# A decoder layer on one Trainium2 core: the forget gate's projection as eight unsplit fp32 products in column groups, and one vector sum moved in the opening

## The chip, the cores and the metric

The kernel runs on one core of one Trainium2 chip. A core has a matrix engine (PE, with its weight loads listed apart as PEld), a vector engine (DVE), a scalar engine (ACT), a general engine (POOL) and a sync engine (SP), which here only issues DMA transfers. The engines run side by side, each through its own queue of instructions in order, and wait for each other by semaphores. The metric is the device time of one execution in microseconds (us).

## What is computed

One decoder layer on 512 tokens of width 1024. A conditioning vector gives six modulation vectors; the token-mixing half applies one combined input projection to the modulated input `u`, runs two causal attention branches of eight heads each, merges and projects them; a gated MLP with a causal convolution follows. The part that matters here is the head of the layer:

```python
mod = c @ w_ada + b_ada
sh1, sc1, gt1, sh2, sc2, gt2 = [m[:, None, :] for m in jnp.split(mod, N_MOD, axis=-1)]
u = x * (1.0 + sc1) + sh1
proj = u @ w_in
q_a, k_a, v_a, f_a, q_b, k_b, v_b, g_a, g_b = jnp.split(proj, _split_points(), axis=-1)
log_f = jax.nn.log_sigmoid((f_a + b_forget).astype(jnp.float32)).transpose(0, 2, 1)
```

`f_a` is the forget gate: eight columns of the projection, one per head of the forgetting attention. Its logarithm is summed along the sequence and enters the logits of that branch, which is the second of the two to run.

## The kernel before, in words

**Products.** Every fp32 product is made of three products of a faster four-byte type, fp32r. An operand is split into a high part (a copy to fp32r on ACT, `hi_of`) and a low part (operand minus high part on DVE, `lo_of`), and the three are high by high, high by low and low by high. A stationary operand of 128 columns and a moving one of 512 make one product of shape 128x512 in one of the eight banks of PSUM.

**The opening** (lines 222 to 383) runs over eight tiles `j` of 128 rows of the contraction. For each tile, SP issues (`first_load`) two blocks of modulation weights `wa[0]`, `wa[1]` of 128x1024, the input weights `r` of 128x904, and the transposed input `xt` of 128x512. `first_acc` makes the tile's shift and scale: `mod_col` multiplies a weight block by the broadcast vector `cbc` and sums it in one DVE instruction (line 241), reads the accumulator, and adds the bias (line 247). `first_mod` then makes `u`: twice on ACT (line 318 into the high part `uh`, line 323 in place into `xt`, unsplit), and `ul = xt - uh` on DVE; the low part `wl` of the weights, 904 columns, is made on DVE just ahead of that. `first_split` makes the high part of the next tile's weights on ACT.

Of the 904 weight columns, seven groups of 128 go to banks `grp[0]` to `grp[6]`: query and key of a first pair of heads and five gate blocks. The last eight columns are the forget gate. `first_pad` splits them once more into a zeroed tile `fpad` of 128 columns per tile: the high part in columns 0 to 7, the low part in columns 64 to 71. `first_ops` then needs two full-width products for them, `fpad` by `uh` and `fpad` by `ul`, both into `grp[7]`. So a tile has 7 x 3 + 2 = 23 products (line 361), and the opening 184.

**The order on PE in the opening** follows `first_mm`: groups 0 to 4, then 5 to 7; in the last tile groups 2, 0, 1, then 7, then 3 to 6. On DVE the explicit order (`issue_after`) per tile is: sum 0 and sum 1 of the tile (`first_acc`), `wl`, `ul`, the low part into `fpad`; the next tile's sums stand behind that. Between other instructions of an engine the order comes from a scheduler that places what it takes to be ready, so an instruction of a later line can stand ahead of one of an earlier line; SP's order is the program's.

**After the opening**, `q_evac` and `k_evac` split the first pair's query and key out of the banks. `forget_evac` (line 405) takes the forget gate out: rows 64 to 71 of `grp[7]` by an ACT copy, then rows 0 to 7 plus the bias plus that copy by DVE, into `fq[1]`. `forget` (line 409) is issued in the loop over heads before the second branch's attention (line 839): an absolute value, an exponential and a logarithm on ACT, a minimum and a running sum on DVE, then a split, and its rows go to the heads by DMAs of POOL. The rest of the projection follows in 128-column blocks, three products for each tile of the contraction (`proj`, `mm3`, lines 152 to 154), mixed with the attention of the heads.

**Buffers.** `xt`, `uh`, `ul`, `fq` and most tiles of the attention come from one pool of 58 tiles of 128x512 (`z`). The modulation weights have five buffers, `r` five, the split weights three.

Of the kernel before, what the change touches and what calls it, by code (L numbers as in the profile page):

```python
# [8 lines left out]
F32 = mybir.dt.float32  # L9
F32R = mybir.dt.float32r  # L10
BF16 = mybir.dt.bfloat16
AF = mybir.ActivationFunctionType
ALU = mybir.AluOpType
# [3 lines left out]
P = 128  # L17
T = 512
D = 1024
KT = D // P  # L20
# [5 lines left out]
NH = 8  # L26
# [25 lines left out]
def layer_kernel(ctx: ExitStack, tc: tile.TileContext, out, xT, x, c8, wa0, wa1, bcol, w1, wct, wv, bf,  # L52
# [3 lines left out]
    V, S, G, PE = nc.vector, nc.scalar, nc.gpsimd, nc.tensor  # L56
# [12 lines left out]
    early = st0.enter_context(tc.tile_pool(name="early", bufs=1))  # L69

    cnt, state = [0], {"load": 0, "proc": 0}

    def nm(s):
        cnt[0] += 1
        return f"{s}_{cnt[0]}"

    def bank():
        return pp.tile([P, 512], F32, name=nm("ps"), tag="ps")
# [5 lines left out]
    def const(shape, dt, s):  # L84
        return cons.tile(shape, dt, name=s, tag=s)

    def fl(ap):
        return ap.bitcast(F32)

    def hi_of(o, i, scale=1.0):  # L90
        S.activation(o, i, AF.Copy, scale=scale)

    def lo_of(o, i, hi):
        state["read"] = V.tensor_tensor(o, i, fl(hi), ALU.subtract)  # L94
        return state["read"]
# [33 lines left out]
    g = G.tensor_copy(crow[0:KT], c8s)  # L129
# [11 lines left out]
    bfs = const([NH, 1], F32, "bfs")  # L141
# [6 lines left out]
    def z(dt, s, shape=(P, 512)):  # L148
        return zp.tile(list(shape), dt, name=nm(s), tag="z", bufs=NZ)
# [73 lines left out]
    grp = [bank() for _ in range(8)]  # L223
    pend = {}

    fpad = early.tile([P, KT, P], F32R, name="fpad", tag="fpad")
    with tc.issue_after(g.ins):
        G.memset(fl(fpad), 0.0)
    def heat(n):
        return [PE.matmul(grp[5], warm[:, 0:P], warm, start=True, stop=True) for _ in range(n)]  # L230

    heat(WARM[0])
    for k in range(KT):
        o = grp[6 + k // 4][:, k % 4 * P : (k % 4 + 1) * P]
        m = PE.matmul(o, sel[:, k : k + 1].broadcast_to([P, P]), ctop, start=True, stop=True)
# [8 lines left out]
    def mod_col(w, col, wt):  # L244
        mod_sum(w, col, wt, slice(0, D), 0)
        b, o = bcols[:, w, col : col + 1], modc[:, w, col : col + 1]
        return V.tensor_tensor(o, modr[:, w, col, 0:1], b, ALU.add)
# [25 lines left out]
    def first_acc(j):  # L273
        wa = pend[j][0]
        if j == 0:
            s = state["chl"]
            for e in range(2):
                for q in range(2):
                    c = slice(q * 512, (q + 1) * 512)
                    with tc.issue_after(s.ins):  # L280
                        s = mod_sum(q, j, wa[e], c, e, grp[6 + e])
                    if e or q:
                        for m in heat(WARM[2] + e * q):
                            paced(m, s)
                    if e and not q:
                        with tc.issue_after(s.ins):
                            s = V.tensor_tensor(bcols[:, 0:2, j], bcols[:, 0:2, j], modr[:, 0:2, j, 0], ALU.add)
            with tc.issue_after(s.ins):
                state["modc"] = V.tensor_tensor(modc[:, 0:2, j], modr[:, 0:2, j, 1], bcols[:, 0:2, j], ALU.add)
        else:  # L290
            mod_col(0, j, wa[0])
            state["modc"] = mod_col(1, j, wa[1])

    def first_split(j):
# [9 lines left out]
    def first_pad(j):  # L304
        h, l, r = pend[j][2:]
        if j == 0:
            c = slice(384, W1C)
            lo_of(l[:, c], r[:, c], h[:, c])
        f = slice(W1C - NH, W1C)
        hi_of(fpad[:, j, 0:NH], r[:, f])  # L310
        state["after"] = lo_of(fpad[:, j, 64 : 64 + NH], r[:, f], h[:, f])

    def first_mod(j):
        wa, xt = pend[j][0:2]
        sh, sc = modc[:, 0, j : j + 1], modc[:, 1, j : j + 1]
        a, b = z(F32R, "uh"), z(F32R, "ul")
        if j:
            u = S.activation(a, xt, AF.Identity, bias=sh, scale=sc)
            h, l, r = pend[j][2:]
            with tc.issue_after(state["modc"].ins):  # L320
                state["after"] = lo_of(l[:, 0:W1C], r[:, 0:W1C], h[:, 0:W1C])
            with tc.issue_after(u.ins):
                u = state["u"] = S.activation(xt, xt, AF.Identity, bias=sh, scale=sc)
            with tc.issue_after(state["after"].ins):
                state["after"] = lo_of(b, xt, a)
        else:
            h, l, r = pend[j][2:]
            with tc.issue_after(state["modc"].ins):
                ts = V.tensor_scalar(a, x0, sc, sh, ALU.mult, ALU.add)
            with tc.issue_after(state["h"].ins):  # L330
                u = S.activation(xt, x0, AF.Identity, bias=sh, scale=sc)
            c = slice(384, W1C)
            with tc.issue_after(u.ins):
                u = S.activation(h[:, c], r[:, c], AF.Copy)
            for e in range(2):
                with tc.issue_after(u.ins):
                    u = state["u"] = S.activation(cbc[:, e * 512 : (e + 1) * 512], grp[6 + e], AF.Copy)
            with tc.issue_after(ts.ins):
                ts = lo_of(l[:, 0:384], r[:, 0:384], h[:, 0:384])
            with tc.issue_after(ts.ins):  # L340
                state["after"] = lo_of(b, xt, a)
        with tc.issue_after(u.ins), tc.issue_after(state["after"].ins):
            first_pad(j)
        uh.append(a)
        ul.append(b)

    def first_ops(j, g):
        h, l = pend[j][2:4]
        a, b = uh[j], ul[j]
        if g == 7:  # L350
            return [(fpad[:, j, :], a), (fpad[:, j, :], b)]
        c = slice(g * P, (g + 1) * P)
        return [(h[:, c], a), (l[:, c], a), (h[:, c], b)]

    def first_mm(j, gs):
        ops = [(g, n, m) for g in gs for n, m in enumerate(first_ops(j, g))]
        if j < KT - 1:
            rank = (0, 2, 4, 1, 3, 5)
            ops.sort(key=(lambda o: rank[o[1]] + 3 * (o[0] > 2) if o[0] < 5 else o[1] + 3 * (o[0] == 7)) if j == 0 else lambda o: o[1] + 3 * (o[0] == 7))
        for g, n, (w, u) in ops:  # L360
            PE.matmul(grp[g], w, u, start=j == 0 and n == 0, stop=j == KT - 1 and n == (1 if g == 7 else 2))  # L361

    for j in range(2):
        first_load(j)
    first_split(0)
    first_acc(0)
    first_mod(0)
    for j in range(KT):
        if j + 2 < KT:
            first_load(j + 2)  # L370
        if j + 1 < KT:
            with tc.issue_after(state["u"].ins):
                first_split(j + 1)
            with tc.issue_after(state["after"].ins):
                first_acc(j + 1)
        if j < KT - 1:
            first_mm(j, range(5))
        if j + 1 < KT:
            first_mod(j + 1)
        if j < KT - 1:  # L380
            first_mm(j, range(5, 8))
        else:
            first_mm(j, (2, 0, 1, 7, 3, 4, 5, 6))

    st0.close()

# [14 lines left out]


    fq = [z(F32, "fq", (NH, 512)) for i in range(2)]

    def forget_evac():
        S.activation(fq[0], grp[7][64 : 64 + NH, :], AF.Copy)
        V.scalar_tensor_tensor(fq[1], grp[7][0:NH, :], bfs, fq[0], ALU.add, ALU.add)

    def forget(after):
        with tc.issue_after(after.ins):  # L410
            S.activation(fq[0], fq[1], AF.Abs)
            S.activation(fq[0], fq[0], AF.Exp, scale=-1.0)
            S.activation(fq[0], fq[0], AF.Ln, bias=1.0)
        V.scalar_tensor_tensor(fq[1], fq[1], 0.0, fq[0], ALU.min, ALU.subtract)
        V.tensor_tensor_scan(fq[0], ones[0:NH, 0:1].broadcast_to([NH, 512]), fq[1], 0.0, ALU.mult, ALU.add)
        hi_of(chi[:, 0, :], fq[0])
        lo_of(chi[:, 1, :], fq[0], chi[:, 0, :])
        gated.append(True)
        for h in range(4):
            if idx(0, h) - 4 in scored:  # L420
                decay_rows(h)
# [18 lines left out]
    def idx(br, h):  # L440
        return h if br == 1 else NH + h
# [314 lines left out]
    for p, nb in (6, 3), (7, 5):  # L756
        add_pair(p)
        for _ in range(nb):
            j = bj.pop(0)
# [260 lines left out]
    for n in range(2 * FT):  # L1020
        wui.append(add_item(wup[n], split_proc))
        if n in GTILES:
            k = GTILES.index(n)
# [11 lines left out]
        if n in (28, 31, 32, 35):  # L1035
            k = (28, 31, 32, 35).index(n)
            w = wdp[FP - 1][:, k * 512 : (k + 1) * 512]
# [54 lines left out]
    hs, ops, s4s = [], [], []  # L1092
# [61 lines left out]
    for n in range(2 * FT):  # L1154
        if n < NSPLIT:
            h, l = items[wui[n]][4]
            ps = bks[n]
            up_mm(ps, h, l, slice(256, 512))
        else:
            ps = bank()  # L1160
            h, l = weights(wui[n], min(LOADS - 1, wui[min(n + 2, 2 * FT - 1)] - wui[n]))
# [27 lines left out]
        if n % 2 == 1:  # L1189
            g, v = hc  # L1190
# [18 lines left out]
    r = x1  # L1209
# [104 lines left out]
    for n, k in enumerate(wi):  # L1314
        w = weights(k)
# [87 lines left out]
```

## Time and profile before

| what | us |
|---|---|
| median of three runs | 736.88 (735.89 to 737.09) |
| the profiled execution, its own time | 736.08 |
| its span in the profile | 734.3 |
| busy in the span: PE / weight loads | 724.3 / 604.8 |
| busy in the span: DVE / ACT / POOL | 599.7 / 390.1 / 84.5 |
| first product of the opening starts | 8.00 |
| first product after the opening starts | 50.22 |

The span is what the profile covers, from the first instruction recorded to the last; 1.8 us of the execution's own time lie around it. PE's busy time is overlapped: the records of successive products cover each other, so a product is best read by the distance from its start to the next one's start. The granted clock of PE is 0.997 of full speed over the span, so no stretch is slowed by it. The fence rows in the next sections have the start in us, the duration in us, the engine, the line of the kernel, the operation, what it writes and reads, its shape and its count; in brackets stands how long the engine was idle before it and what ended that.

### The profile page before, as it was taken

The page shows a single profiled execution, that of the slowest core. Times are in us where ns is not written, and L with a number is a line of the kernel's source. Part 1 is how long each engine was busy: PE and PEld are TensorE (multiplying, and loading weights), DVE is VectorE, ACT ScalarE, POOL GpSimd, SP SyncE. Part 2 cuts the span into 40 slices and gives each one's busy share as a digit, 9 for nine tenths or more (in the row PEclk, how much of TensorE's full clock was granted, in tenths as well). Part 3 has the DMA queues.
Part 4 walks back from the last instruction along what each step waited for, and adds up shares of the span by engine and source line. Part 5 has one row for each costly group of instructions (what it writes and reads, how often), then busy time and mean ns, then how long its engine had stood idle before and what let it go on. Part 6 is the DMA issues. An engine that isn't in the chain of part 4 may idle for free.

```text
span 734.3 us, 9843 instructions
## 1 busy us (share of the span) xinstructions
PE 724.3 (99%) x3442; PEld 604.8 (82%) x3442; DVE 599.7 (82%) x1049; ACT 390.1 (53%) x681; POOL 84.5 (12%) x140
## 2 busy tenths in 40 slices
PE   8999999999999999999999999999999999999995
PEld 5888888888888888888889888888888888888885
DVE  7878799778899896883697999977887878679996
ACT  5576466596885755432065644444453544346550
POOL 1026224343010000000000001000011001000010
PEclk9999999999999999999999999999999999999998
DMA  9944534523332242632075687577799767656734
GB/s 351 404 167 147 196 116 160 185 65 119 135 117 79 95 153 77 206 145 86 1 258 134 218 249 230 177 242 229 206 345 248 212 224 212 214 168 219 228 83 92
DMA packets 45203, 131.96 MB, mean 180 GB/s; under 512 B 6137, under 2 KB 6657, under 8 KB 45153
## 3 DMA queue, kind: packets, MB, share of 16 engines
q1 hardware_dynamic: 37888, 112.61, 44.3%
q0 software_dynamic: 4224, 10.30, 7.4%
q10 hardware_dynamic: 3040, 8.42, 3.1%
q8 instruction: 27, 0.44, 0.2%
q14 instruction: 24, 0.19, 0.1%
HBM read 118.39 MB, written 12.85 MB: 179 GB/s over the span
## 4 chain that ended last, share of the span: by engine, by line
PE 98%; DVE 1%; DMA 0%; issue 0%; DVEq 0%
PE ps L152 19%; PE ps L154 19%; PE ps L153 19%; PE ps L361 6%; PE ps L1131 5%; PE ps L1133 5%; PE ps L1132 5%; PE ps L599 3%; PE ps L581 2%; PE ps L507 2%; PE ps L509 2%; PE ps L508 2%; PE ps L924 2%; PE ps L922 2%; PE ps L923 2%; PE ps L533 1%
## 5 line engine op out<-in xcount | busy, mean ns | idle before, releaser
L217 ACT ACTIVATE wh<-raw 128x1024 fp32r<-128x1024 f32 (+1 forms) x105 | 109.2, 1042 | 107.4 <-PE ps L153 35.2
L94 DVE TENSOR_TENSOR wl<-raw,wh 128x1024 fp32r<-128x1024 f32 (+2 forms) x114 | 137.8, 1210 | 34.2 <-ACT wh L217 33.5
L152 PE MATMUL ps<-u2h,wh 128*128 128x512 f32 (+1 forms) x376 | 141.3, 376 | 0.0
L153 PE MATMUL ps<-u2l,wh 128*128 128x512 f32 (+1 forms) x376 | 141.2, 375 | 0.0
L154 PE MATMUL ps<-u2h,wl 128*128 128x512 f32 (+1 forms) x376 | 141.2, 375 | 0.0
L154 PEld LDWEIGHTS ps<-u2h,wl 128*128 128x128 f32 x376 | 70.8, 188 | 12.9
L152 PEld LDWEIGHTS ps<-u2h,wh 128*128 128x128 f32 x376 | 70.8, 188 | 12.7
L153 PEld LDWEIGHTS ps<-u2l,wh 128*128 128x128 f32 x376 | 70.8, 188 | 12.7
L152 PE MATMUL ps<-uh,wh 128*128 128x512 f32 x200 | 79.5, 398 | 0.0
L154 PE MATMUL ps<-uh,wl 128*128 128x512 f32 x200 | 78.3, 391 | 0.0
L153 PE MATMUL ps<-ul,wh 128*128 128x512 f32 x200 | 77.9, 390 | 0.0
L1184 ACT ACTIVATE cv<-ps,cw 128x512 f32<-128x512 f32 x44 | 34.0, 773 | 46.2 <-PE ps L154 36.2
L1185 DVE SCALAR_TENSOR_TENSOR cv<-ps,cw,cv 128x511 f32<-128x511 f32 x44 | 32.8, 745 | 22.6 <-ACT cv L1184 22.5
L154 PEld LDWEIGHTS ps<-uh,wl 128*128 128x128 f32 x200 | 37.5, 188 | 8.6 <-DVE wl L94 0.3
L153 PEld LDWEIGHTS ps<-ul,wh 128*128 128x128 f32 x200 | 37.6, 188 | 7.5
L152 PEld LDWEIGHTS ps<-uh,wh 128*128 128x128 f32 x200 | 37.5, 188 | 7.3
L241 DVE SCALAR_TENSOR_TENSOR raw<-raw,cbc 128x1024 f32<-128x1024 f32 x32 | 39.6, 1238 | 0.0
L561 POOL TENSOR_TENSOR pt<-pt,om 128x127 f32<-128x127 f32 (+3 forms) x32 | 38.5, 1213 | 1.6 <-DVE om L560 1.5
L181 POOL DMA_DIRECT2D raw<-in_wdp x10 | 8.8, 884 | 245.1 <-DMA raw<-in_wdp 208.4
L1186 DVE SCALAR_TENSOR_TENSOR cv<-ps,cw,cv 128x510 f32<-128x510 f32 x44 | 32.7, 743 | 0.4
L1192 ACT ACTIVATE cv<-cv 128x512 f32<-128x512 f32 x22 | 13.9, 631 | 34.1 <-DVE cv L1186 34.1
L560 DVE TENSOR_TENSOR_SCAN om<-om,dg 128x127 f32<-128x127 f32 (+3 forms) x32 | 27.1, 907 | 2.9 <-ACT om L555 2.9
(238 smaller groups left out, 1552.5 us busy)
## 6 DMA issues: line engine op xcount, KB each, us to landing
raw<-in_wup SPq DMA_DIRECT2D x44, 512.0 KB, 4.7
raw<-in_wa SPq DMA_DIRECT2D x32, 512.0 KB, 3.5
raw<-in_wct SPq DMA_DIRECT2D x25, 512.0 KB, 4.5
raw<-in_wdp SPq DMA_DIRECT2D x20, 512.0 KB, 5.6
wa<-in_wa SPq DMA_DIRECT2D x16, 512.0 KB, 8.6
raw<-in_wdp SPq DMA_DIRECT2D x22, 256.0 KB, 4.5
raw<-t SPq DMA_DIRECT2D x22, 256.0 KB, 4.1
raw<-in_wdp POOLq DMA_DIRECT2D x10, 512.0 KB, 7.4
```

Source lines behind the costliest of these rows:

```text
L94: state["read"] = V.tensor_tensor(o, i, fl(hi), ALU.subtract)
L152: PE.matmul(ps, wh, ah, start=first, stop=False)
L153: PE.matmul(ps, wh, al, start=False, stop=False)
L154: return PE.matmul(ps, wl, ah, start=False, stop=last)
L217: state["hi"] = S.activation(h[:, 0:cols], r[:, 0:cols], AF.Copy)
L241: state["read"] = V.scalar_tensor_tensor(wt[:, c], wt[:, c], 1.0, cbc[:, c] if by is None else by, ALU.mult, ALU.mult, accum_out=o)
L361: PE.matmul(grp[g], w, u, start=j == 0 and n == 0, stop=j == KT - 1 and n == (1 if g == 7 else 2))
L561: G.tensor_tensor(pt[b][:, s : e - 1], pt[b][:, s : e - 1], om[:, s + 1 : e], ALU.mult)
L1131: PE.matmul(ps, ah, bh, start=first, stop=False, skip_group_check=onto)
L1132: PE.matmul(ps, ah, bl, start=False, stop=False, skip_group_check=onto)
L1133: return PE.matmul(ps, al, bh, start=False, stop=last, skip_group_check=onto)
L1184: S.activation(t, ps, AF.Identity, bias=cw[:, n, 3:4], scale=cw[:, n, 2:3])
```

## The change

There are two parts. **The forget gate.** The padded tile `fpad` and its memset on POOL go. The eight columns are copied by ACT as plain fp32 into a small tile `fw`, and no low part is made of them. The unsplit `u` (the tile `xt` after line 323) is kept, in a list `us`. In place of two products in each of eight tiles there are eight products of type fp32 in the last tile, behind groups 2, 0 and 1: eight stationary columns, 512 moving columns, product `k` at column group `32 * (k % 4)` of the array and so in rows 0, 32, 64 or 96 of `grp[7]`. Products 0 to 3 start the four sums and products 4 to 7 add to them. Taking the gate out of the bank then needs three ACT copies in place of one, and `forget` has two more sums, on POOL.

**The order on DVE.** From tile 1 on, `mod_col(0, j + 1)`, the next tile's first sum, is issued between `wl` and `ul` of tile `j`; before, it stood behind `ul` and the low part into `fpad`. `first_acc` keeps only the second sum, except for tile 1.

```diff
-    fpad = early.tile([P, KT, P], F32R, name="fpad", tag="fpad")
-    with tc.issue_after(g.ins):
-        G.memset(fl(fpad), 0.0)
+    fw = early.tile([P, KT, NH], F32, name="fw", tag="fw")
+    us = []
...
-            mod_col(0, j, wa[0])
+            if j == 1:
+                mod_col(0, j, wa[0])
             state["modc"] = mod_col(1, j, wa[1])
...
-            lo_of(l[:, c], r[:, c], h[:, c])
+            state["after"] = lo_of(l[:, c], r[:, c], h[:, c])
         f = slice(W1C - NH, W1C)
-        hi_of(fpad[:, j, 0:NH], r[:, f])
-        state["after"] = lo_of(fpad[:, j, 64 : 64 + NH], r[:, f], h[:, f])
+        hi_of(fw[:, j, :], r[:, f])
...
+            if j + 1 < KT:
+                with tc.issue_after(state["after"].ins):
+                    state["after"] = mod_col(0, j + 1, pend[j + 1][0][0])
             with tc.issue_after(state["after"].ins):
                 state["after"] = lo_of(b, xt, a)
...
+        us.append(xt)
...
-        if g == 7:
-            return [(fpad[:, j, :], a), (fpad[:, j, :], b)]
...
+    def forget_mm(m):
+        for k in range(KT):
+            q = 32 * (k % 4)
+            with tc.issue_after(m.ins):
+                m = PE.matmul(grp[7][q : q + NH, :], fw[:, k, :], us[k], start=k < 4, stop=k > 3, tile_position=(0, q))
+        return m
...
-            first_mm(j, range(5, 8))
+            first_mm(j, range(5, 7))
         else:
-            first_mm(j, (2, 0, 1, 7, 3, 4, 5, 6))
+            forget_mm(first_mm(j, (2, 0, 1)))
+            first_mm(j, range(3, 7))
...
     fq = [z(F32, "fq", (NH, 512)) for i in range(2)]
+    parts = [fq[0]] + [z(F32, "fp", (NH, 512)) for i in range(2)]
...
-        S.activation(fq[0], grp[7][64 : 64 + NH, :], AF.Copy)
-        V.scalar_tensor_tensor(fq[1], grp[7][0:NH, :], bfs, fq[0], ALU.add, ALU.add)
+        for q in range(3):
+            S.activation(parts[q], grp[7][32 * q + 32 : 32 * q + 32 + NH, :], AF.Copy)
+        V.scalar_tensor_tensor(fq[1], grp[7][0:NH, :], bfs, parts[0], ALU.add, ALU.add)
 
     def forget(after):
+        G.tensor_tensor(parts[1], parts[1], parts[2], ALU.add)
+        G.tensor_tensor(fq[1], fq[1], parts[1], ALU.add)
         with tc.issue_after(after.ins):
```

More of the change, by code (lines that the diff above doesn't have):

```diff
@@ L358, in first_mm @@
             rank = (0, 2, 4, 1, 3, 5)
-            ops.sort(key=(lambda o: rank[o[1]] + 3 * (o[0] > 2) if o[0] < 5 else o[1] + 3 * (o[0] == 7)) if j == 0 else lambda o: o[1] + 3 * (o[0] == 7))
+            ops.sort(key=(lambda o: rank[o[1]] + 3 * (o[0] > 2) if o[0] < 5 else o[1]) if j == 0 else lambda o: o[1])
         for g, n, (w, u) in ops:
-            PE.matmul(grp[g], w, u, start=j == 0 and n == 0, stop=j == KT - 1 and n == (1 if g == 7 else 2))
+            m = PE.matmul(grp[g], w, u, start=j == 0 and n == 0, stop=j == KT - 1 and n == 2)
+        return m
     for j in range(2):
```

## The prediction

> **What bounds the kernel now.** I read the page's busy times and its chain of work first, then the windows of the opening cut at each tile's first product, then the timelines of PE, DVE and ACT there.
>
> ```profile
> PE 724.3 (99%) x3442; PEld 604.8 (82%) x3442; DVE 599.7 (82%) x1049; ACT 390.1 (53%) x681; POOL 84.5 (12%) x140
> PE 98%; DVE 1%; DMA 0%; issue 0%; DVEq 0%
> 8.00 42.38 PE ps L361 x184
> 18.67:23.92 5.25, 5.25 (x24) 4.32 (x23) 4.27 (x9) 2.89 (x5) 0.00 (x0) 1.00 1.03 405
> 23.92:29.17 5.25, 5.25 (x24) 4.32 (x23) 4.37 (x10) 2.82 (x7) 0.00 (x0) 1.00 1.03 401
> ```
>
> PE makes 98% of the chain, and the chain holds all 184 products of the opening in one piece: 42.38/184 = 0.230 us each. In the windows (length, then busy time of PE, PEld, DVE, ACT, POOL, granted clock, DMA share, GB/s) PE is full and the clock 1.00. So time leaves this kernel where products leave PE, if the next thing that PE needs comes early enough. Two others are near: DMA, whose share is 1.03 in both windows, and the loop through DVE and ACT, below.
>
> **What is removed.**
>
> ```profile
> 23.00 0.61 PE L361 MATMUL ps<-ul,wh 128*128 128x512 f32 x2
> 23.45 0.40 PE L361 MATMUL ps<-uh,fpad 128*128 128x512 f32 x1
> 23.69 0.39 PE L361 MATMUL ps<-ul,fpad 128*128 128x512 f32 x1
> 23.92 1.32 PE L361 MATMUL ps<-uh,wh 128*128 128x512 f32 x5
> 12.64 0.19 PEld L361 LDWEIGHTS ps<-uh,fpad 128*128 128x128 f32 x1
> 12.86 0.40 PE L361 MATMUL ps<-uh,fpad 128*128 128x512 f32 x1
> 13.29 0.99 PEld L361 LDWEIGHTS ps<-uh,wh 128*128 128x128 f32 x5 [0.24 <-ACT uh L318]
> 13.33 1.39 PE L361 MATMUL ps<-uh,wh 128*128 128x512 f32 x5
> ```
>
> From start to start the two padded products of a tile cost 23.92 - 23.45 = 0.47. Without them a tile costs 5.25 - 0.47 = 4.78. Eight tiles would give 3.76. Tile 0 gives nothing: its pair runs from 12.86 to 13.33, and the weight load behind it already waited 0.24 for `uh` of tile 1. That `uh` starts on ACT when the split of tile 1's weights ends, and this waited for its load:
>
> ```profile
> 11.57 0.96 ACT L91 ACTIVATE wh<-raw 128x904 fp32r<-128x904 f32 x1 [1.87 <-DMA raw<-in_w]
> 12.44 0.80 ACT L318 ACTIVATE uh<-xt,modc 128x512 fp32r<-128x512 f32 x1
> ```
>
> The change moves no load and nothing ahead of these on ACT, so PE will idle from about 12.86 to 13.33. Gain: 7 x 0.47 = **3.29**.
>
> **Does the rest of a tile keep up with 4.78?**
>
> ```profile
> 24.78 1.21 DVE L241 SCALAR_TENSOR_TENSOR wa<-wa,cbc 128x1024 f32<-128x1024 f32 x1
> 25.94 1.23 DVE L241 SCALAR_TENSOR_TENSOR wa<-wa,cbc 128x1024 f32<-128x1024 f32 x1
> 27.28 1.10 DVE L94 TENSOR_TENSOR wl<-raw,wh 128x904 fp32r<-128x904 f32 x1
> 29.10 0.69 DVE L94 TENSOR_TENSOR ul<-xt,uh 128x512 fp32r<-128x512 f32 x1 [0.72 <-ACT xt L323]
> 29.71 0.16 DVE L94 TENSOR_TENSOR fpad<-raw,wh 128x8 fp32r<-128x8 f32 x1
> 29.79 1.22 DVE L241 SCALAR_TENSOR_TENSOR wa<-wa,cbc 128x1024 f32<-128x1024 f32 x1
> ```
>
> DVE's round is 29.79 - 24.78 = 5.01. In the old order it would be the new bound: 4.78 < 5.01. The moved sum (1.16 from start to start, with about 0.1 for its bias) goes into the 0.72 in which DVE waits for `xt`, and the `fpad` row (0.08) goes. New round: 5.01 - 0.72 - 0.08 = 4.21. The move issues no DMA, and passes no SP or POOL instruction. What it pushes back is `ul`. At tile 1, the first, `wl` ends near 13.6, the sum and its bias near 14.9, `ul` near 15.6:
>
> ```profile
> 15.71 1.29 PE L361 MATMUL ps<-ul,wh 128*128 128x512 f32 x5
> 14.66 0.96 ACT L91 ACTIVATE wh<-raw 128x904 fp32r<-128x904 f32 x1 [0.48 <-DMA raw<-in_w]
> 15.95 1.22 DVE L241 SCALAR_TENSOR_TENSOR wa<-wa,cbc 128x1024 f32<-128x1024 f32 x1
> 17.41 0.82 ACT L318 ACTIVATE uh<-xt,modc 128x512 fp32r<-128x512 f32 x1 [1.78 <-DVE modc L247]
> wa<-in_wa SPq DMA_DIRECT2D x16, 512.0 KB, 8.6
> raw<-in_w SPq DMA_DIRECT2D x7, 452.0 KB, 8.0
> xt<-in_xT SPq DMA_DIRECT2D x7, 256.0 KB, 8.7
> ```
>
> PE wants it at 15.71, so it is in time by 0.1. The loads: a tile takes 2 x 512 + 452 + 256 KB = 1.77 MB, at 405 GB/s 4.38 us, less than 4.78, so from tile 3 on the loads gain on PE. Tile 2 is the tight one. Its `raw` landed at 14.66 (the wait of ACT); the second `wa` block follows in the queue, 0.52 MB or 1.29 later, at an estimated 15.95, which is when DVE read it anyway. So `uh` of tile 2 comes no earlier than now, 17.41 + 0.82 = 18.23, while PE would be free at 13.33 + 4.78 = 18.11 and its first row there stands some 0.04 behind its input. Cost 0.1 at tile 2, and none after it: **0.1**.
>
> **What is added on PE.** No fp32 product of unsplit operands and none in a column group is in this trace; the price has to be bounded.
>
> ```profile
> 52.94 0.22 PE L532 MATMUL ps<-m,s 128*128 128x128 f32 x1
> 52.99 0.28 PE L533 MATMUL ps<-m,s 128*128 128x128 f32 x1
> 70.52 1.25 PE L581 MATMUL ps<-ident,pt 128*128 128x128 f32 x10
> 71.52 0.48 PE L507 MATMUL ps<-wh,uh 128*128 128x512 f32 x1
> 71.84 0.39 PE L508 MATMUL ps<-wl,uh 128*128 128x512 f32 x1
> ```
>
> The only unsplit operands on PE are in the transposes: ten of 128 columns take 71.52 - 70.52 = 1.00, so 0.10 each, against 0.05 (52.99 - 52.94) for an fp32r product of that width. From below, then, one to two fp32r times, 0.23 to 0.46. From above: high and low parts make four partial products, of which this kernel computes three at 0.23; a unit that keeps all four needs 4 x 0.228 = 0.91. I take 0.91, because a type that were cheaper would make the split of the whole kernel needless. The Trainium skill, "FP8 and Floating Point Precision", section "TensorE Precision Notes", also has true fp32 in four passes; no run here shows it.
>
> How far do four column groups overlap? From full overlap, two rounds, 2 x 0.91 = 1.82, to none, 8 x 0.91 = 7.28. I take full overlap, since each group has its own columns, its own PSUM rows and no shared sum. The two changes of the array's shape: a product's record is 0.39 long but the next starts 0.23 later, so a pipeline that has to run empty costs 0.16, twice 0.32; at the nearest change of kind, transposes to products, the first takes 71.84 - 71.52 = 0.32 in place of 0.23, so 0.09 extra. Ends 0 and 2 x (0.16 + 0.19 of an uncovered weight load) = 0.7. Added: 1.82 + 0.32 = **2.14**. The Trainium skill, "TensorE: Matmul & The Clock Gate", section "Part 3: Packing small matmuls — row/col tiling", reports 2.38x for three column tiles of 512 columns: by that the eight would take about 7.28/3.17 = 2.3 (2.38 x 4/3 = 3.17), an estimate from its figure. No run here shows it.
>
> **What else is added.**
>
> ```profile
> 50.67 0.59 ACT L406 ACTIVATE fq<-ps 8x512 f32<-8x512 f32 x1
> 51.16 1.04 ACT L217 ACTIVATE wh<-raw 128x1024 fp32r<-128x1024 f32 x1
> 53.71 0.60 ACT L555 ACTIVATE om<-ps 128x512 f32<-128x512 f32 x1 [1.50 <-PE ps L533]
> 59.67 1.08 POOL L561 TENSOR_TENSOR pt<-pt,om 128x511 f32<-128x511 f32 x1
> ```
>
> Two more copies on ACT, 51.16 - 50.67 = 0.49 each, stand ahead of a weight split and of the first sigmoids, which wait 1.50 for PE: cover 1.50 against 0.98. This work also starts some 2.8 earlier against groups 0 to 2 and PE's next use of it is only 1.1 earlier, so cover grows. Without it, at most 1.0. Two sums on POOL, 1.08 each by the row, are idle-time work if they are placed when their inputs are ready, about 50. Eight `xt` tiles live to the end of the opening, where 24 of the pool's 58 are held. Nothing: 0.
>
> **Sum.** -3.29 + 0.1 + 2.14 = -1.05. From the profiled execution's 736.08 that is **735.0**. This execution lies 0.8 below the median of 736.88, inside the runs' range; from the median the sum gives 735.8.
>
> **The rivals.** *Groups in series.* If a product enters the array as several passes and passes start in queue order, a pass of one group holds back all behind it. With two double passes of 0.46, each group overlaps its neighbour by one: 9 x 0.46 + 0.32 = 4.46, so -3.19 + 4.46 = +1.3, 737.4. With four single passes: 25 x 0.228 + 0.32 = 6.02, +2.8, 738.9; with no overlap 7.6, +4.4, **740.5**. This is the case on the other side: the change breaks even at 3.2 for the eight products, a spacing of 0.36 from one product to the next, where full overlap has 0.23. For it speaks that in the whole trace no two products of PE overlap by more than their tails; against it, that none of them ever had a part of the array for itself. The Trainium skill (same page and section) has matmuls start strictly in order, which fits the series and does not decide how many passes there are.
>
> *The loop stays the bound.* If the moved sum only delays `ul`, or the loads come late, the tile's round stays near 5.01: six tiles give back 6 x 0.23 = 1.4, +0.3, 736.4. Against it speaks the wait of 0.72 on DVE that the sum fills.
>
> *ACT held by POOL.* If POOL's sums are placed by their line,
>
> ```profile
> 151.39 3.89 POOL L561 TENSOR_TENSOR pt<-pt,om 128x127 f32<-128x127 f32 x3
> 155.28 1.09 POOL L561 TENSOR_TENSOR pt<-pt,om 128x511 f32<-128x511 f32 x1
> 152.04 0.62 ACT L411 ACTIVATE fq<-fq 8x512 f32<-8x512 f32 x1
> ```
>
> they end near 156.4 + 2.2 = 158.6, and line 411 holds ACT 6.5, with the splits of the next head and weights behind it; some of that, say 3, reaches PE: 738. Against it, the scheduler places what is ready, and POOL's row at 151 shows it idle long before.
>
> **How the numbers follow.** Full overlap 0.53; with its unknowns (product of three or four passes, switches 0 to 0.7) it spans -3.19 + 1.37 = -1.8 to -3.19 + 2.52 = -0.7, so 734.3 to 735.4, or 736.2 from the median. Double passes in order 0.15; the loop 0.10; single passes or no overlap 0.17; ACT held 0.05. A measurement of this kernel can tell about 0.2%, 1.5 us, from no change. Of full overlap I put 0.25 beyond -1.5 and 0.28 within; double passes and the loop are within: same 0.53. Single passes, no overlap and ACT held: slower 0.22. The range leaves out those 0.22: 734.0 (the lower end) to 738.2 (double passes, from the median: 736.88 + 1.3).
>
> **What would show it.** Right: tiles 1 to 6 of 4.78 from first product to first product, a gap of about 0.47 on PE before 13.33, DVE's round no longer waiting for `xt`, eight narrow products within 2.1 or so, the first product of line 152 near 49.2. Wrong: narrow products spaced over 0.36; a tile near 5.0; line 411 waiting for POOL. The forecast falls above all with the overlap of the groups.

## The result, and the profile after

| what | before | after |
|---|---|---|
| median of 22 runs, us | 735.91 (735.54 to 738.24) | 735.08 (734.57 to 736.45) |
| ratio, with its 95% interval | | 0.9988 (0.9983 to 0.9994) |
| profiled execution, own time / span, us | 736.08 / 734.3 | 734.73 / 733.0 |

The changed kernel is faster by 0.12%, or 0.83 us between the medians: a real gain, and less than 0.2%. The forecast was 735.0 with a sum of -1.05. The median of the kernel before is from more runs here than in the table of the time before, which had three.

The page after the change, first the busy times by engine, then the chain of work by engine:

```profile
PE 723.3 (99%) x3442; PEld 602.2 (82%) x3442; DVE 601.0 (82%) x1041; ACT 391.0 (53%) x683; POOL 87.6 (12%) x141
PE 97%; DVE 1%; DMA 0%; ACT 0%; issue 0%; DVEq 0%
```

PE has as many instructions as before, 3442: sixteen padded products have gone and sixteen records have come, two for each fp32 product. PE is still the chain. The next view has the opening of the changed kernel cut at each tile's first product, and its last stretch at the first product after the opening (start and end, length, then busy times of PE, PEld, DVE, ACT, POOL, the granted clock, DMA share, GB/s). The last row is the sum of the same view of the kernel before, cut in the same way.

```profile
7.79:12.91 5.12, 5.02 (x21) 3.83 (x21) 4.88 (x10) 3.45 (x8) 0.00 (x0) 1.00 1.03 414
12.91:17.87 4.96, 4.96 (x21) 3.84 (x22) 4.55 (x9) 2.72 (x5) 0.00 (x0) 1.00 1.03 408
17.87:22.74 4.87, 4.87 (x22) 4.03 (x22) 4.80 (x10) 3.11 (x5) 0.00 (x0) 1.00 1.03 406
22.74:27.50 4.76, 4.76 (x22) 3.94 (x21) 4.36 (x9) 2.98 (x6) 0.00 (x0) 1.00 1.04 405
27.50:32.39 4.89, 4.89 (x22) 3.75 (x20) 3.81 (x8) 1.79 (x3) 0.00 (x0) 1.00 1.02 401
32.39:37.29 4.90, 4.90 (x23) 4.05 (x22) 4.83 (x10) 3.14 (x5) 1.52 (x4) 1.00 1.04 408
37.29:42.05 4.76, 4.76 (x23) 3.94 (x21) 3.87 (x8) 3.03 (x6) 2.34 (x5) 1.00 1.03 409
42.05:49.08 7.03, 7.03 (x38) 4.13 (x37) 4.07 (x6) 6.64 (x12) 0.00 (x0) 1.00 0.31 103
```

```profile
sum 42.22, PE 42.22 PEld 34.54 DVE 34.20 ACT 25.66 POOL 3.86; mean PE 5.28 PEld 4.32 DVE 4.28 ACT 3.21 POOL 0.48
```

| tile | 0 | 1 | 2 | 3 | 4 | 5 | 6 | 7 | sum |
|---|---|---|---|---|---|---|---|---|---|
| before, us | 5.33 | 5.34 | 5.25 | 5.25 | 5.26 | 5.25 | 5.25 | 5.29 | 42.22 |
| after, us | 5.12 | 4.96 | 4.87 | 4.76 | 4.89 | 4.90 | 4.76 | 7.03 | 41.29 |
| difference | -0.21 | -0.38 | -0.38 | -0.49 | -0.37 | -0.35 | -0.49 | +1.74 | -0.93 |
| forecast | 0 | -0.47 | -0.37 | -0.47 | -0.47 | -0.47 | -0.47 | +1.67 | -1.05 |

So the opening is 0.93 shorter, and apart from tile 0 in the places that were named. Tile 0 is no gain of the change: in the eight profiles of this study that have the fp32 products it takes 5.12 to 5.52, on average 5.33, which is what it took before. It ends with `uh` of tile 1, for which ACT waits for a load (it starts the split of that load at 11.14 here and at 11.74 in the second profile of this kernel, below). The granted clock is 1.00 in all of the opening; the stretch that the mean of 0.997 hides in the kernel before is its last 14.3 us, at 0.83. The spans differ by 1.3; 0.21 of the rest is that this execution's first product started at 7.79 and not at 8.00. In the other profiles of this study it starts between 7.72 and 8.90, with no part of the change ahead of it, so this is not counted as an effect.

The timeline of PE after the change, at the first boundary, at tile 2, at tile 5, and in tile 7:

```profile
12.20 0.61 PE L369 MATMUL ps<-ul,wh 128*128 128x512 f32 x2
12.91 1.45 PE L369 MATMUL ps<-uh,wh 128*128 128x512 f32 x5
14.20 1.31 PE L369 MATMUL ps<-uh,wl 128*128 128x512 f32 x5
17.87 1.40 PE L369 MATMUL ps<-uh,wh 128*128 128x512 f32 x5
19.11 1.07 PE L369 MATMUL ps<-uh,wl 128*128 128x512 f32 x4
...
32.39 1.43 PE L369 MATMUL ps<-uh,wh 128*128 128x512 f32 x5
...
43.18 0.39 PE L369 MATMUL ps<-uh,wl 128*128 128x512 f32 x1
43.50 0.96 PE L369 MATMUL ps<-ul,wh 128*128 128x512 f32 x3
44.39 1.90 PE L360 MATMUL ps<-xt,fw 128*8 128x512 f32 x16
46.23 0.50 PE L369 MATMUL ps<-uh,wh 128*128 128x512 f32 x1
46.56 0.39 PE L369 MATMUL ps<-uh,wl 128*128 128x512 f32 x1
```

And the weight loads of the fp32 products:

```profile
44.39 0.12 PEld L360 LDWEIGHTS ps<-xt,fw 128*8 128x8 f32 x8 [0.36 <-issue]
44.83 0.11 PEld L360 LDWEIGHTS ps<-xt,fw 128*8 128x8 f32 x4 [0.32 <-issue]
45.26 0.11 PEld L360 LDWEIGHTS ps<-xt,fw 128*8 128x8 f32 x4 [0.32 <-issue]
```

The eight products stand from 44.39 to 46.23, 1.84. Their sixteen weight loads come as eight and then twice four, 0.43 apart, and the sixteen records of the products start in fours, at 44.39 and then every 0.43. So four groups work at once, and each takes four passes of 0.43, two for each of its two products. The block's edges are short: the three `ul` products take 0.89 with a stretched first (below), so 0.09 is left ahead of the block at most, and the product behind it takes 46.56 - 46.23 = 0.33 in place of 0.23.

On DVE, POOL and ACT after the change:

```profile
19.88 1.23 DVE L240 SCALAR_TENSOR_TENSOR wa<-wa,cbc 128x1024 f32<-128x1024 f32 x1
21.23 1.10 DVE L94 TENSOR_TENSOR wl<-raw,wh 128x904 fp32r<-128x904 f32 x1
22.25 1.22 DVE L240 SCALAR_TENSOR_TENSOR wa<-wa,cbc 128x1024 f32<-128x1024 f32 x1
23.59 0.68 DVE L94 TENSOR_TENSOR ul<-xt,uh 128x512 fp32r<-128x512 f32 x1
24.24 1.23 DVE L240 SCALAR_TENSOR_TENSOR wa<-wa,cbc 128x1024 f32<-128x1024 f32 x1
15.51 1.22 DVE L240 SCALAR_TENSOR_TENSOR wa<-wa,cbc 128x1024 f32<-128x1024 f32 x1 [0.34 <-DMA wa<-in_wa]
30.06 1.22 DVE L240 SCALAR_TENSOR_TENSOR wa<-wa,cbc 128x1024 f32<-128x1024 f32 x1 [1.01 <-DMA wa<-in_wa]
```

```profile
50.06 1.82 POOL L422 TENSOR_TENSOR fp<-fp,fp 8x512 f32<-8x512 f32 x1 [8.05 <-ACT fp L418]
51.95 2.15 POOL L423 TENSOR_TENSOR fq<-fq,fp 8x512 f32<-8x512 f32 x1
```

```profile
52.57 0.60 ACT L569 ACTIVATE om<-ps 128x512 f32<-128x512 f32 x1 [1.65 <-PE ps L547]
```

`ul` has no bracket any more: the moved sum fills the wait for `xt`. The second sum of tile 2 (15.51) now waits 0.34 for its load, and that of tile 5 (30.06) 1.01: at these two places DVE has come as far as the loads allow. Behind the second of them `uh` of tile 5 is late by 0.13 for PE. POOL's sums run at 50, as soon as their inputs are there, and behind the three copies the sigmoids still wait 1.65 for PE, where they waited 1.50 before, so the copies hold nothing up there.

### The profile page after: what moved, and what is told of

Its sections match the earlier page's. It is cut to its first block, busy times and chain, and to the rows that moved or that the text cites. A ratio compares the mean times of both kernels' runs of the same rounds, so it can differ in the third digit from the quotient of the medians.

```text
span 733.0 us, 9836 instructions
## 1 busy us (share of the span) xinstructions
PE 723.3 (99%) x3442; PEld 602.2 (82%) x3442; DVE 601.0 (82%) x1041; ACT 391.0 (53%) x683; POOL 87.6 (12%) x141
## 4 chain that ended last, share of the span: by engine, by line
PE 97%; DVE 1%; DMA 0%; ACT 0%; issue 0%; DVEq 0%
PE ps L152 19%; PE ps L154 19%; PE ps L153 19%; PE ps L1145 5%; PE ps L1146 5%; PE ps L1147 5%; PE ps L369 5%; PE ps L613 3%; PE ps L595 2%; PE ps L521 2%; PE ps L523 2%; PE ps L522 2%; PE ps L938 2%; PE ps L937 2%; PE ps L936 2%; PE ps L547 1%
## 5 line engine op out<-in xcount | busy, mean ns | idle before, releaser
L574 DVE TENSOR_TENSOR_SCAN om<-om,dg 128x127 f32<-128x127 f32 (+3 forms) x32 | 28.8, 962 | 3.6 <-ACT om L569 3.6
```

## The experiments

All ratios are against the kernel before, measured beside each kernel on the same chip, with 95% intervals.

**The changed kernel with the old order on DVE.**

```diff
-            if j + 1 < KT:
-                with tc.issue_after(state["after"].ins):
-                    state["after"] = mod_col(0, j + 1, pend[j + 1][0][0])
...
-            if j == 1:
-                mod_col(0, j, wa[0])
+            mod_col(0, j, wa[0])
```

> The changed kernel with the old order on DVE: both modulation sums of a tile stand behind the low part of u again; the forget gate stays eight fp32 products. If the moved sum was needed: DVE's round is the old 5.01 less 0.08, so 4.93, and a tile of the opening takes about 4.93 from its first product to the next tile's, where the changed kernel has 4.76 to 4.96 (mean of tiles 1 to 6: 4.86) and PE alone 4.76; DVE again waits some 0.7 for xt in each tile; the gain of 0.9 against the kernel before falls to about 0.4 (ratio 0.9995). If the old order was no bound: tiles as in the changed kernel, ratio 0.9988.

Ratio 1.0000 (0.9991 to 1.0008). From its timeline of DVE, and of PE at the first products of tiles 3 and 4:

```profile
22.07 1.10 DVE L94 TENSOR_TENSOR wl<-raw,wh 128x904 fp32r<-128x904 f32 x1
23.88 0.69 DVE L94 TENSOR_TENSOR ul<-xt,uh 128x512 fp32r<-128x512 f32 x1 [0.71 <-ACT xt L321]
```

```profile
23.08 1.40 PE L365 MATMUL ps<-uh,wh 128*128 128x512 f32 x5
27.96 1.43 PE L365 MATMUL ps<-uh,wh 128*128 128x512 f32 x5
```

The wait of 0.71 for `xt` is back and the tile takes 27.96 - 23.08 = 4.88 (tiles 1 to 6: 4.99, 4.94, 4.88, 4.92, 4.91, 4.91, mean 4.93, as expected). PE has two products less to do and waits for the loop instead. The opening takes 42.16, 0.87 more than in the changed kernel; 0.41 of that is tiles 1 to 6, and 0.31 is tile 0 (5.43 against 5.12, ahead of which nothing differs), which varies as much between profiles; the rest is tile 7 (7.18 against 7.03), and is not settled. The plain case for the loop is tiles 3 to 6, 4.88 to 4.92, where PE alone takes 4.76. The gain expected, 0.4, lies within the interval, and so does none.

**The kernel before with the new order alone.**

```diff
+            if j + 1 < KT:
+                with tc.issue_after(state["after"].ins):
+                    state["after"] = mod_col(0, j + 1, pend[j + 1][0][0])
...
-            mod_col(0, j, wa[0])
+            if j == 1:
+                mod_col(0, j, wa[0])
```

> The kernel before with the moved sum alone; the padded products stay. If PE bounds the opening of the kernel before: tiles 1 to 6 stay at 5.25, the first product after the opening stays near 50.2, ratio 1.0000 (0.9995 to 1.0005). If the order itself brings the gain: tiles below 5.2 and a ratio near 0.999.

Ratio 0.9996 (0.9988 to 1.0005). The opening takes 42.15, from 8.06 to 50.21, against 42.22: PE had no wait in it to lose. So neither half by itself shows a gain that can be told from none (0.06 and 0.07 of the opening, less than tile 0 varies), and both together give 0.93.

**All eight products in one column group.**

```diff
-            q = 32 * (k % 4)
...
-                m = PE.matmul(grp[7][q : q + NH, :], fw[:, k, :], us[k], start=k < 4, stop=k > 3, tile_position=(0, q))
+                m = PE.matmul(grp[7][0:NH, :], fw[:, k, :], us[k], start=k == 0, stop=k == KT - 1, tile_position=(0, 0))
...
-        for q in range(3):
-            S.activation(parts[q], grp[7][32 * q + 32 : 32 * q + 32 + NH, :], AF.Copy)
-        V.scalar_tensor_tensor(fq[1], grp[7][0:NH, :], bfs, parts[0], ALU.add, ALU.add)
+        S.activation(fq[1], grp[7][0:NH, :], AF.Identity, bias=bfs)
...
-        G.tensor_tensor(parts[1], parts[1], parts[2], ALU.add)
-        G.tensor_tensor(fq[1], fq[1], parts[1], ALU.add)
```

> The changed kernel with all eight fp32 products in the first column group, one sum; one ACT instruction takes it out with the bias, and the sums on POOL go. If the four groups run beside each other in the changed kernel (16 passes in four sets of four, 0.435 apart): 16 passes one after the other, 7.0 for the eight products in place of 1.84, so +5.1 against the changed kernel, +4.2 against the kernel before, ratio 1.0057. If the products are cheap by themselves (a pass of eight columns near the 0.23 of an fp32r product): 16 x 0.23 = 3.7, +1.8 against the changed kernel, ratio 1.0012.

Ratio 1.0141 (1.0126 to 1.0157), 10.7 us above the kernel before, where +4.2 was expected. PE's timeline:

```profile
44.54 7.03 PE L359 MATMUL ps<-xt,fw 128*8 128x512 f32 x16
51.50 0.50 PE L368 MATMUL ps<-uh,wh 128*128 128x512 f32 x1
54.38 0.39 PE L152 MATMUL ps<-uh,wh 128*128 128x512 f32 x1
```

The block is as expected, 51.50 - 44.54 = 6.96 for sixteen passes, and the opening, from 8.09 to 54.38, takes 46.29, +4.1 against the kernel before. The other 6.6 are lost far behind it. From its timeline of ACT, the pieces of its chain of work other than PE, and its windows at 190 and 195:

```profile
182.37 0.61 ACT L420 ACTIVATE fq<-fq 8x512 f32<-8x512 f32 x1
```

```profile
192.68 3.63 DMA m<-chi
```

```profile
190.00:195.00 5.00, 2.51 (x14) 1.85 (x12) 3.08 (x5) 2.97 (x3) 2.86 (x6) 1.00 0.50 186
195.00:200.00 5.00, 3.23 (x9) 2.50 (x10) 2.68 (x9) 2.35 (x9) 2.28 (x5) 0.69 0.13 34
```

The scheduler has put the forget gate's functions at 182, not at 150; the rows that POOL's DMA brings to the second branch land at 196.3, and PE stands idle for 4.3 of those ten us; in the second five its granted clock is 0.69. The remainder of the 6.6 is not traced, and why the order moved is open. What counts for the block is its own 6.96. Its products share the sum as well as the columns, so the runs do not say which of the two makes them go one after the other.

**The eight products made twice.**

```diff
-        for k in range(KT):
+        for k in list(range(KT)) * 2:
```

> The changed kernel with the eight products made twice; the second time starts the sums anew, so the result is the same. If each round of four groups costs two passes of 0.435: 1.74 more, eight sets of passes instead of four, +0.85 against the kernel before, ratio 1.0011. If the 1.84 of the block is mostly the two changes of the array's shape: under 0.9 more, ratio at most 1.0000.

Ratio 1.0009 (1.0001 to 1.0018). PE's timeline:

```profile
44.41 3.62 PE L360 MATMUL ps<-xt,fw 128*8 128x512 f32 x32
47.96 0.50 PE L369 MATMUL ps<-uh,wh 128*128 128x512 f32 x1
```

The block takes 3.55, 1.71 more than 1.84. So of the 1.84 only 0.13 is the block's own edge and the rest is passes; the rival of a block that is mostly switching falls.

**Neighbours in the same group.**

```diff
-            q = 32 * (k % 4)
+            q = 32 * (k // 2)
...
-                m = PE.matmul(grp[7][q : q + NH, :], fw[:, k, :], us[k], start=k < 4, stop=k > 3, tile_position=(0, q))
+                m = PE.matmul(grp[7][q : q + NH, :], fw[:, k, :], us[k], start=k % 2 == 0, stop=k % 2 == 1, tile_position=(0, q))
```

> The changed kernel with products 0 and 1 in the first column group, 2 and 3 in the second, and so on, so that neighbours in the order share a group; the same four sums and the same way out of the bank. If each group takes its passes as its own column is free, whatever stands between them: 16 passes over four groups again, block 1.84, time as the changed kernel (ratio 0.9988). If a product that finds its group busy holds back all that stand behind it: passes of one group in series, the next group beside only the last of them: 13 passes of 0.435, block 5.7, +3.8 against the changed kernel, ratio 1.004.

Ratio 0.9985 (0.9977 to 0.9994), as the changed kernel. PE's timeline:

```profile
45.27 1.92 PE L360 MATMUL ps<-xt,fw 128*8 128x512 f32 x16
47.12 0.50 PE L369 MATMUL ps<-uh,wh 128*128 128x512 f32 x1
```

The block takes 1.85 in this order too, and not the 5.7 of the second case. A product whose group is busy does not hold those behind it, at least over these sixteen passes. With the block of 1.84, against 4.46 and more for groups in series, that rival has no form left that these runs allow.

**The changed kernel once more.**

> The changed kernel once more, beside the others of this call: ratio 0.9988, opening from first to first product after it 41.3 where the kernel before has 42.2; whether the wait for a late load in tile 5 (0.13 on PE) comes again tells whether it belongs to the change.

Ratio 0.9992 (0.9983 to 1.0000); the opening, from 7.94 to 49.22, takes 41.28. PE does not wait at tile 5 here, and tiles 3 to 6 take 4.76 each. The load is no earlier, though. The second sum of tile 5 on DVE:

```profile
30.07 1.23 DVE L240 SCALAR_TENSOR_TENSOR wa<-wa,cbc 128x1024 f32<-128x1024 f32 x1 [0.43 <-DMA wa<-in_wa]
```

It starts at 30.06 in the first profile and at 30.07 here, both times when its load lands. What differs is PE: tile 0 takes 5.52 here and 5.12 there, so PE comes to tile 5 at 32.85 and not at 32.39. The 0.13 comes again in the profile of the kernel with POOL's late sums (last experiment), whose tile 0 ends at 12.94, as early as in the first profile (12.91; here at 13.46). The kernel before comes to tile 5 only at 34.43. So the wait belongs to the change: where tile 0 ends early, PE catches up with the loads at tile 5 and gives time back there and in tile 7, and the two openings end up equal, 41.28 and 41.29.

**The split behind the opening moved back on ACT.**

```diff
-            with tc.issue_after(state["k" if state["proc"] else "after"].ins):
+            with tc.issue_after(state["k" if state["proc"] else "after"].ins), tc.issue_after(state["u"].ins):
```

> The changed kernel with the first weight split after the opening put behind the unsplit u of tile 7 on ACT, where it stood ahead of it: the low part of u in tile 7 comes about 1.0 earlier, PE's gap of 0.1 before its first product with it goes. At most 0.1 to gain, 0.01%: ratio as the changed kernel, 0.9987. If the later split is missed elsewhere: the first products after the opening wait for its low part, some 0.3 to 1.0 lost.

Ratio 0.9998 (0.9989 to 1.0007), against 0.9992 of the changed kernel measured beside it: no gain, and the intervals overlap too far to call it a loss. `ul` of tile 7 did come earlier, at 41.93, but PE's order changed with it and put a product that needs it third:

```profile
42.30 0.39 PE L369 MATMUL ps<-uh,wl 128*128 128x512 f32 x1
42.68 0.50 PE L369 MATMUL ps<-ul,wh 128*128 128x512 f32 x1
```

The long step has moved from 43.18, where the next start came 0.32 later, to 42.30, where it comes 0.38 later; without a wait it is 0.23. In the second profile of the changed kernel PE comes to tile 7 later and has no such wait, so there was little to gain.

**POOL's sums by their place in the code.**

```diff
+        with tc.issue_after(state["pool"].ins):
-        G.tensor_tensor(parts[1], parts[1], parts[2], ALU.add)
-        G.tensor_tensor(fq[1], fq[1], parts[1], ALU.add)
+            G.tensor_tensor(parts[1], parts[1], parts[2], ALU.add)
+            G.tensor_tensor(fq[1], fq[1], parts[1], ALU.add)
```

(`state["pool"]` is the last product of POOL in `stage_a`.)

> The changed kernel with the two sums on POOL ordered behind the products of POOL that stand ahead of forget in the code, which end near 154.3 in the changed kernel. They took 1.82 and 2.15 there, so they end near 158.3, and the absolute value on ACT, at 150.0 now, cannot start before. If ACT's queue is held behind it and no cover is there: some 3 to 8 us on PE, ratio 1.003 to 1.010. If the order on ACT has the splits ahead of it or the second branch's gate rows have slack: ratio as the changed kernel, 0.9988.

Ratio 1.0079 (1.0065 to 1.0093): 6.0 us above the kernel before, and 7.0 above the changed kernel measured beside it (734.97). From its timelines of POOL and ACT and its windows:

```profile
166.69 1.29 POOL L423 TENSOR_TENSOR fp<-fp,fp 8x512 f32<-8x512 f32 x1
168.05 1.28 POOL L424 TENSOR_TENSOR fq<-fq,fp 8x512 f32<-8x512 f32 x1
```

```profile
169.36 0.63 ACT L426 ACTIVATE fq<-fq 8x512 f32<-8x512 f32 x1 [5.92 <-POOL fq L424]
```

```profile
175.00:180.00 5.00, 3.50 (x17) 2.79 (x16) 3.89 (x8) 4.20 (x8) 0.00 (x0) 1.00 0.10 13
180.00:185.00 5.00, 2.44 (x16) 1.74 (x14) 4.92 (x9) 2.52 (x7) 0.00 (x0) 1.00 0.52 200
```

The sums were expected to end near 158.3; they end at 169.3, because products of POOL for one more head stand ahead of them. ACT stands 5.92 behind one instruction that waits for POOL, the splits of the next head and weights come late, and PE idles 1.50 + 2.56 = 4.1 in the ten us shown. The time of the changed kernel hangs on the sums being done early, at 50.

## Why the prediction was right

*PE is the bound, and products that leave it leave the time.* Right: tiles 3 and 6, where nothing waits, are 4.76 against 5.25.

*Tile 0 gives nothing.* Right on average (5.33 in eight profiles). In the first profile PE idles from 12.65 (12.20 and two slots of 0.23) to 12.91, 0.26 and not 0.47, because `uh` of tile 1 came 0.2 earlier after the first product than before; in the second profile it idles 0.66, from 12.80 to 13.46. The load of tile 1 decides that, not the change.

*The moved sum is needed, and fits into the wait for `xt`.* Right in both directions: without it the tile is 4.93, and it earns nothing where PE is the bound. The forecast of the round, 4.21, became 4.36 (the starts of the second sums, 19.88 and 24.24), with no wait in it. Each sum is now followed by a bias of its own, 1.35 and 1.34 to the next instruction where the two took 27.28 - 24.78 = 2.50; the prediction named this 0.1 and left it out of the round.

*Tile 2 is the tight one, 0.1, and none after it.* The first half is right: the first five products of tile 2 take 19.11 - 17.87 = 1.24 in place of 1.13. Tile 1 was not named and loses as much: its first five take 1.29, behind the wait at 12.91. The second half failed: the loads were to gain on PE from tile 3 on, at 4.38 for a tile. The second weight block of tile 5 lands 14.55 behind that of tile 2 (15.51 and 30.06), so 4.85 for a tile, and 4.66 in the second profile. In the first profile PE pays 0.13 for the wait at tile 5 and 0.14 in the five products behind it. Why these loads come so late is open.

*Eight products at 0.91, in two rounds beside each other, and 0.32 of switching: 2.14.* A product takes 2 x 0.43 = 0.87, two rounds and the edges 1.84, and with the gap ahead and the longer product behind it (0.09 + 0.10) 2.03. The bound from below, one or two fp32r times, was far off; the kernel's own three products for one, 3 x 0.23 = 0.68, were the better guide to what an unsplit one must cost. Sixteen passes in one group take 6.96, in four 1.84: a factor of 3.8. The Trainium skill's 2.38x for three column tiles ("TensorE: Matmul & The Clock Gate", section "Part 3: Packing small matmuls — row/col tiling") is lower than this in proportion, and here the measurement decides. Its rule that matmuls start strictly in order, read so that a product with a busy group holds those behind it, would give 5.7 where neighbours share a group, and 1.85 was measured; the records do not name their product, so the order itself is not seen.

*The copies on ACT are covered, and POOL's sums run when they are ready.* Right, with a size off: POOL's sums took 1.82 and 2.15, not 1.08. The rival, ACT held by POOL, is real and was priced at 3 on top of the forecast: forced, it costs 7.0 against the changed kernel.

*The sum.* What was mis-sized in it is small and of both signs: in the first profile the block 0.1 too dear, tile 0 0.2 too pessimistic, and some 0.5 not foreseen in tiles 1, 4 and 5 and in tile 7's wait for `ul`. In tile 7 the scheduler had put a split of 1.04 ahead of `xt` on ACT. The sum, -1.05, met -0.93 in the opening and -0.83 between the medians. That 735.0 lies within 0.1 of the measured 735.08 is partly luck: the start, 736.08, lay 0.17 above the later median, which hid most of the 0.22 by which the sum was too large. Nor could the time alone decide for full overlap, since the range of 734.0 to 738.2 held double passes (737.4) and the loop (736.4) as well; the tiles of 4.76 and the block of 1.84 do.

## What to carry to other kernels

When work leaves the bound engine, look at once for the loop that comes next and compare its round with the new one: here neither of two edits shows a gain by itself, and both together give 0.12%. Look also at how far behind the loads are: a tile that PE finishes sooner reaches them sooner. Narrow products of full fp32 need not be split and padded to the array's width: with eight columns and four column groups they run four at a time. And a side computation with long slack can still hold a shared queue: here the place of two small sums on an otherwise idle engine decided 7 us.

## What the runs showed of the hardware that was not expected

- An fp32 product of 128 x 8 by 512 columns is two records on PE, 0.43 from start to start in one column group, where an fp32r product is one of 0.23; its weight loads take 0.09 where 128 columns take 0.19. Four column groups run at once, in either order (1.84 and 1.85 for the block).
- A wait of PE costs more than its length: behind the one at 12.91 five products take 1.29 in place of 1.13, and behind the one at 32.39 they take 1.27. Behind the block of fp32 products, without a wait, the next takes 0.33 in place of 0.23.
- The same sum of 8 x 512 on POOL took 1.82 and 2.15 while DVE was busy at 50 to 54, and 1.29 and 1.28 where DVE did next to nothing (165 to 170, in the kernel with the late sums). DVE's split beside the second one took 1.54 where such a split takes 1.22. The Trainium skill ("SBUF — State Buffer", section "🔬 SBUF: two separate sides") has the two engines share a pair of ports that one of them holds for a whole instruction when both read two operands; the numbers go that way, but no run separates it.
